# The first blocks of an encoder step: x and the modulation weights read by feature block, and three weight blocks begun on two of three token tiles

## The chip, the cores and the metric

The kernel runs on one core of a Trainium2 chip. Its engines work beside each other, each through an instruction queue of its own: TensorE (PE; its weight loads are listed as PEld), VectorE (DVE), ScalarE (ACT), GpSimd (POOL), and SyncE (SP), which issues most DMA transfers. They wait for one another by semaphores. What counts is the device time of one execution in microseconds. The time before is the median of three runs, 1598.21 us (1597.47 to 1599.44).

## The reference, cut to what matters

One inference step: one trunk layer on a prompt of 1024 tokens and on a sample of 32, with its own modulation row `c` for each of the two.

```python
mod = jax.nn.silu(c) @ w_ada + b_ada
sh1, sc1, gt1, sh2, sc2, gt2 = jnp.split(mod[:, None, :], 6, axis=-1)
h = rmsnorm(x, g_mix) * (1 + sc1) + sh1
u = h @ w_in
qa, ka, va, qm, km, vm, om, ip, fp, ga, gm = jnp.split(u, _split_points(), axis=-1)
...                    # band attention (qa, ka, va), mLSTM (qm .. fp), gates (ga, gm)
x = x + gt1 * (merged @ w_out)
...                    # rmsnorm, SwiGLU, residual, final rmsnorm
```

The change touches the part up to the first three column blocks of `u`: `rmsnorm` needs the mean square of each token over all 1024 features, and `sc1` and `sh1` need `silu(c) @ w_ada` over the first 2048 columns of `w_ada`.

## The kernel before, in words

Features lie on the 128 partitions, in eight blocks (`KD` = 8); tokens run along the free axis, 1024 of the prompt and then 32 of the sample, 1056 in all, in three tiles of 352 columns (`TILES`). A matrix product in f32 precision is made of three products of high and low parts (`PASSES`): weights and inputs are split into a high part (written by ACT) and the low remainder (by DVE or POOL). One weight block of 128 output columns on one tile therefore takes 8 x 3 products of 128x352. `unit()` (L436) makes these 24 for one tile and lets side work (attention, then the mLSTM) put its own instructions between them; `k` counts feature blocks.

**The front.** SP loads x by tokens: eight transfers of 128 tokens and one of the 32 sample tokens (L216 to L223). DVE sums the squares of each (L273), PE transposes x in 64 pieces of 128x128 (L281) and 8 of the sample, ACT copies the results into `xTs`. POOL takes the power -1/2 of the mean squares, and `bcast_cols` (L234) spreads the result over the partitions as `RB`. Then `load_ada` has eight transfers of 1 MB, rows of `w_ada` by input feature `k`. For each, PE adds the scale part into PSUM (L322, 128 columns wide, the two modulation rows side by side) and DVE accumulates the shift part in SBUF (L312, L314); at the end PE sums the shift over the partitions (`row_sums`, L348 and L352). Only with the eighth transfer is any scale known, for all feature blocks at once. `first_scale` and `first_shift` finish both; `scaled_x` (L375, DVE), `high_h` (L386, ACT) and `low_h` (L392 DVE for the prompt, L394 POOL for the sample's 32 columns) make the two parts of `h`. xT is also stored to DRAM (`xres`, L1508), and read back for the residual after attention.

**The first products.** `first_units` (L467) takes the first two weight blocks, K and V of head pair 0 (`KA`, `VA`), on all three tiles: 2 x 3 x 3 = 18 products for each `k`, 144 in all (L475), with one feature block at a time as `h` is made. The six sums fill six PSUM banks. Then Q of head pair 0 (`QA`) follows by `unit()`: 72 products (L443). After these come the blocks of head pair 1, with attention of pair 0 beside them as side work: scores (L725), bias added and maximum taken by DVE (L739), exponentials by ACT (L740) and scaled by POOL (L745), transposes (L752), products with V (L783).

**Orders and buffers.** The order on PE, ACT, DVE and POOL is that in which the code is written; the order of SP's transfers is chosen by a scheduler. Each weight block is loaded into one of three `wraw` buffers (512 KB; L419 via `weight`) and split into `wsp` or, where `home` is `slots`, elsewhere; early in the program the low part is POOL's (L410). A `wraw` buffer is free once its split is done, and a load that waits for one holds up what stands behind it in SP's queue. `W.loaded` and `W.split_n` count blocks loaded and split; `W.advance()` splits and loads as far as `W.ahead` and the buffers allow. The attention's bias tiles come from `rb_d` in DRAM (L691), and POOL clears two corners of each (L692, L693). DVE and ACT split the cached K and V of the sample (`cache_kv`: L684, L602, L603) as one of the jobs in `side.later`, which `unit()` takes one at a time.

Of the kernel before, what the change touches and what calls it, by code (L numbers as in the profile page):

```python
# [139 lines left out]
def hybrid_stream_step(  # L140
    ctx: ExitStack,
    tc: tile.TileContext,
    x_prompt, x_sample, cache_k, cache_v, state_conv, state_C, state_n, state_m,
# [9 lines left out]
    xp, xs_in = x_prompt[0], x_sample[0]  # L153
    w_in, w_ada, w_out, w_down = w_in[0], w_ada[0], w_out[0], w_down[0]
# [40 lines left out]
    def f(ap):  # L195
        return ap.bitcast(F32)
# [11 lines left out]
    ssq = cp.tile([P, NB], F32, name="ssq")  # L208
    pool.memset(ssq, 1.0)
# [4 lines left out]
    xtok = []  # L214

    for i in range(KD):  # L216
        if i % 2 == 0:
            xt = slot([P, 2, D])
            xtok += [xt[:, 0], xt[:, 1]]
        sp.dma_start(xtok[i], xp[i * P:(i + 1) * P])  # L220
    pool.dma_start(cols, params)
    xsm = tmpt((TS, D))
    sp.dma_start(xsm, xs_in)  # L223


# [23 lines left out]
    rstd = cp.tile([P, NB], F32, name="rstd")  # L249
    xres = dr.tile([KD, P, T], F32, name="xres")  # L250
    xTs, xTp, xns = [], [], []
    for j in range(KD):
        if j % 2 == 0:
            xT2 = slot([P, 2, T])
            xTp.append(xT2)
        xTs.append(xT2[:, j % 2])

    was = []
    first_ws, first_cols = [], (KA, VA)

    def load_ada(n):
        while len(was) < n:
            wa = slot([P, 2048])
            sp.dma_start(wa, w_ada[len(was) * P:(len(was) + 1) * P, 0:2048])
            was.append(wa)

    load_ada(KD)

    def square_sum(i):
        n = P if i < 8 else TS  # L270
        src = xtok[i] if i < 8 else xsm
        junk = tmpt((P, D), BF16)
        dve.tensor_tensor_reduce(junk[:n], src, src, 1.0, 0.0, ALU.mult, ALU.add, ssq[:n, i:i + 1])  # L273

    def x_transposes(g, j):

        pt = mmt()
        for n in range(2):
            for i in range(2):
                at = (2 * n + i) * P  # L280
                pe.transpose(pt[:, at:at + P], xtok[2 * g + i][:, (j + n) * P:(j + n + 1) * P], ident)  # L281
        act.activation(xTp[j // 2][:, :, g * 256:(g + 1) * 256], pt.rearrange("p (n t) -> p n t", n=2), AF.Copy)

    for g in range(4):
        for i in range(2):
            square_sum(2 * g + i)
        for j in range(0, KD, 2):
            x_transposes(g, j)
        if g == 2:
            param_cols()  # L290
    square_sum(8)
    for j0 in range(0, KD, 4):
        pt = mmt()
        for j in range(j0, j0 + 4):
            pe.transpose(pt[:, (j - j0) * TS:(j - j0 + 1) * TS], xsm[:, j * P:(j + 1) * P], ident[:TS, :TS])
        for j in range(j0, j0 + 4):
            act.activation(xTs[j][:, S:T], pt[:, (j - j0) * TS:(j - j0 + 1) * TS], AF.Copy)
    pool.tensor_scalar(ssq, ssq, 1.0 / D, EPS, op0=ALU.mult, op1=ALU.add)
    pool.tensor_tensor(rstd, ssq, mhalf[:, :NB], op=ALU.pow)
    RB = tmpt()  # L300

    psH, psA = ps_v(), ps_t()
    acv = [tmpt((P, D)) for _ in range(2)]
    sum_at = [psH, psA[:, 512:]]

    def shift_part(k, c, a, b):
        o, w, x = acv[c][:, a * P:b * P], was[k][:, a * P:b * P], csil[:, k, c:c + 1]  # L310
        if k == 0:
            dve.tensor_scalar(o, w, x, None, op0=ALU.mult)  # L312
        else:
            dve.scalar_tensor_tensor(o, w, x, o, op0=ALU.mult, op1=ALU.add)  # L314

    def first_ada():
        first_load()
        for k in range(KD):
            for b in range(KD):
                out = psA[:, b * P:(b + 1) * P]  # L320
                c = csil[:, k].unsqueeze(1).to_broadcast([P, DH, 2])
                pe.matmul(out.rearrange("p (r c) -> p r c", c=2), was[k][:, D + b * P:D + (b + 1) * P], c,  # L322
                          start=(k == 0 and b % 4 == 0), stop=(k == KD - 1), skip_group_check=True)
            if k < KD - 1:
                for c in range(2):
                    shift_part(k, c, 0, KD)
            else:
                shift_part(k, 0, 0, 2)
                shift_part(k, 1, 0, 2)
                shift_part(k, 0, 2, KD)  # L330
            if k == 0:
                bcast_cols(RB, rstd, [P] * 8 + [TS], 0)

    def first_load():

        for _ in range(2):
            first_ws.append(wraw.tile([P, KD, P], F32, tag="wraw", name=nm("wraw")))
        for half in range(2):
            for raw, c in zip(first_ws, first_cols):
                sp.dma_start(raw[:, 4 * half:4 * half + 4], w_in[512 * half:512 * half + 512, c:c + P].rearrange(  # L340
                    "(k p) c -> p k c", p=P))
        W.loaded = 2
        W.load(3)

    def row_sums(c, a, b):
        for b in range(a, b):
            at = (b % 4) * P + c * DH
            pe.matmul(sum_at[b // 4][:, at:at + DH], acv[c][:, b * P:(b + 1) * P],  # L348
                      ones[:, 0:1].to_broadcast([P, DH]), start=(c == 0 and b % 4 == 0), stop=True,
                      skip_group_check=True)  # L350
            if c == 1 and b >= 2:
                pe.matmul(sum_at[b // 4][:, at:at + DH], was[KD - 1][:, b * P:(b + 1) * P],  # L352
                          csil[:, KD - 1, 1:2].to_broadcast([P, DH]), start=False, stop=True, skip_group_check=True)
# [4 lines left out]
    def first_shift(a, b):
        p3 = sum_at[a // 4].rearrange("p (b c r) -> p c b r", c=2, r=DH)[:, :, a % 4:a % 4 + b - a, 0]
        dve.tensor_tensor(sh1[:, :, a:b], p3, cols[:, R_ADA + a:R_ADA + b].unsqueeze(1).to_broadcast([P, 2, b - a]),  # L360
                          op=ALU.add)
# [8 lines left out]
    def scaled_x(j, lo=0, hi=T):  # L370
        if j % 2 == 0 and lo == 0:
            xn2 = slot([P, 2, T])
            xns.extend([xn2[:, 0], xn2[:, 1]])
        for c, a, b in col_segments(lo, hi):
            dve.scalar_tensor_tensor(xns[j][:, a:b], xTs[j][:, a:b], s1[:, c, j:j + 1], RB[:, a:b], op0=ALU.mult,  # L375
                                     op1=ALU.mult)

    def high_h(j, lo=0, hi=T):

        if lo == 0:  # L380
            hs.append(slot([P, 2, T], F32R))
        for c, a, b in col_segments(lo, hi):
            x = xns[j][:, a:b]
            if c == 1:
                act.activation(x, x, AF.Identity, bias=sh1[:, c, j:j + 1])
            act.activation(hs[j][:, 0, a:b], x, AF.Identity, bias=sh1[:, c, j:j + 1] if c == 0 else 0.0)  # L386

    def low_h(j, lo=0, hi=T):
        for c, a, b in col_segments(lo, hi):
            x, o, h = xns[j][:, a:b], hs[j][:, 1, a:b], f(hs[j][:, 0, a:b])  # L390
            if c == 0:
                dve.scalar_tensor_tensor(o, x, sh1[:, c, j:j + 1], h, op0=ALU.add, op1=ALU.subtract)  # L392
            else:
                pool.tensor_tensor(o, x, h, op=ALU.subtract)  # L394
# [72 lines left out]
    def first_units(ws):  # L467

        S = ps_s()
        pts = [[mmt() for _ in TILES], [S[:, :512], S[:, 512:], psA[:, :512]]]  # L470
# [1795 lines left out]
```

## Time and profile before

| | us |
|---|---|
| median of three runs | 1598.21 |
| the profiled execution's own time | 1597.75 |
| its span in the trace | 1596.1 |
| x landed (end of the sample's transfer in the chain of waits) | 15.25 |
| w_ada landed (end of its piece of the chain) | 35.81 |

Read the profile as follows. All times count from the start of the span. A row of a group gives line, engine, operation, output and inputs by the program's names, shapes and count, then the busy time, the mean of one in ns, and the idle time before them with what ended it. A row of the timeline begins with start and duration; in brackets stands what the engine waited for. A piece of the chain of waits, which leads from the last instruction back to the first, gives start, duration and what ran. PE's matmuls are pipelined, so the last one of a burst shows a tail of some 0.3 us that the next work overlaps.

### The profile page before, as it was taken

Reading aid. Unit: us, or ns where it says so; the run is one execution under the profiler, and the core shown is the slowest. Engines: PE = TensorE matmul, PEld = TensorE weight load, DVE = VectorE, ACT = ScalarE, POOL = GpSimd, SP = SyncE. Lnnn points to the kernel's source line nnn. Section 1 sums busy time; section 2 is a strip of 40 time slices with the busy share of each in tenths; the row PEclk is TensorE's granted clock in tenths of the full one; section 3 lists DMA queues with packets and bytes.
Section 4 is the critical chain, followed back from the end, with each engine's and each line's share of the span. In section 5 each row is a group of like instructions: output and inputs, shape, how many; then the busy total and the mean of one; then the engine's idle time right before and its main releaser. Section 6 shows DMA issues by size and latency. Waiting matters only on the chain.

```text
span 1596.1 us, 27244 instructions
## 1 busy us (share of the span) xinstructions
PE 1566.1 (98%) x10167; PEld 1546.2 (97%) x10167; DVE 1126.4 (71%) x2291; ACT 790.5 (50%) x1735; POOL 420.0 (26%) x433
## 2 busy tenths in 40 slices
PE   7999999999999999999999999999999999999997
PEld 6989999999999999999999999999999999999997
DVE  7766555556776845546654699899888886799755
ACT  3665463544555545444433655544544444545443
POOL 0343242433222411000012100565565650000000
PEclk9999999999999999999999999999999999999999
DMA  9823323343132332675443311213222227427444
GB/s 364 265 83 94 98 82 109 86 135 110 43 94 67 88 86 75 133 257 176 133 145 112 106 54 54 95 57 103 81 80 94 68 78 252 143 80 249 130 136 155
DMA packets 209569, 193.48 MB, mean 121 GB/s; under 512 B 11530, under 2 KB 179118, under 8 KB 208414
## 3 DMA queue, kind: packets, MB, share of 16 engines
q1 hardware_dynamic: 206894, 189.92, 38.5%
q8 instruction: 80, 1.31, 0.4%
q10 hardware_dynamic: 2512, 1.77, 0.4%
q14 instruction: 51, 0.42, 0.1%
q0 software_dynamic: 32, 0.06, 0.0%
HBM read 153.24 MB, written 41.63 MB: 122 GB/s over the span
## 4 chain that ended last, share of the span: by engine, by line
PE 91%; DVE 3%; ACT 2%; DMA 2%; issue 1%; SPq 0%; POOL 0%; ACTq 0%; DVEq 0%; POOLq 0%
PE mm L443 41%; PE psb L1811 18%; PE mm L1811 11%; PE psb L2193 3%; PE mm L878 3%; PE mm L2193 2%; PE psV L783 2%; PE psb L2057 2%; PE psS L725 2%; PE psT L752 1%; DMA s<-in_w_ada_dram 1%; PE mm L2057 1%; DMA t<-in_x_sample_dram 1%; PE psV L1112 1%; PE mm L475 1%
## 5 line engine op out<-in xcount | busy, mean ns | idle before, releaser
L443 PE MATMUL mm<-s,wsp 128*128 128x352 f32 x4104 | 687.0, 324 | 0.0
L443 PEld LDWEIGHTS mm<-s,wsp 128*128 128x128 f32 x4104 | 657.3, 188 | 1.8 <-issue 0.4
L410 DVE TENSOR_TENSOR wsp<-wraw,wsp 128x512 fp32r<-128x512 f32 (+1 forms) x280 | 235.6, 858 | 114.1 <-ACT wsp L409 103.1
L1811 PE MATMUL psb<-s,wsp 128*128 128x352 f32 x1611 | 271.7, 322 | 1.6 <-DVE wsp L410 0.9
L409 ACT ACTIVATE wsp<-wraw 128x512 fp32r<-128x512 f32 x336 | 199.5, 617 | 142.4 <-PE psb L1811 44.5
L1811 PEld LDWEIGHTS psb<-s,wsp 128*128 128x128 f32 x1611 | 260.5, 188 | 2.1 <-DVE wsp L410 1.1
L1811 PE MATMUL mm<-s,wsp 128*128 128x352 f32 x933 | 159.3, 322 | 0.0
L1811 PEld LDWEIGHTS mm<-s,wsp 128*128 128x128 f32 x933 | 151.2, 188 | 0.5 <-DVE wsp L410 0.5
L745 POOL TENSOR_SCALAR st<-st,mx 128x640 f32<-128x640 f32 (+5 forms) x72 | 53.1, 738 | 186.2 <-DVE mx L744 171.2
L1207 DVE CUSTOM_DVE_ANT_0 junk<-wa,t 128x512 bf16<-128x512 f32 x128 | 94.7, 740 | 3.1 <-DMA wa<-in_w_mod_dram 2.1
L410 POOL TENSOR_TENSOR wsp<-wraw,wsp 128x512 fp32r<-128x512 f32 x56 | 74.9, 1357 | 57.1 <-ACT wsp L409 55.6
L739 DVE CUSTOM_DVE_ANT_0 st<-psS,bias 128x640 f32<-128x640 f32 (+5 forms) x72 | 44.5, 618 | 57.1 <-PE psS L725 41.9
L740 ACT ACTIVATE st<-st,mx 128x640 f32<-128x640 f32 (+5 forms) x72 | 47.9, 666 | 63.4 <-DVE mx L739 62.3
L1758 POOL TENSOR_TENSOR t<-t,sl 128x352 f32<-128x352 f32 x19 | 18.4, 969 | 212.8 <-ACT sl L1756 212.8
L759 ACT ACTIVATE pT<-psT 128x640 fp32r<-128x640 f32 (+3 forms) x80 | 38.7, 493 | 62.6 <-PE psT L752 47.6
L2166 POOL TENSOR_TENSOR fst<-fst,mhalf 128x6 f32<-128x6 f32 x1 | 2.3, 2312 | 221.1 <-DVE fst L2165 221.1
L764 DVE TENSOR_TENSOR pT<-psT,pT 128x640 fp32r<-128x640 f32 (+3 forms) x80 | 44.0, 558 | 22.2 <-ACT pT L759 22.2
L1420 POOL TENSOR_TENSOR wraw<-wraw,raw 128x512 f32<-128x512 f32 x33 | 55.8, 1705 | 0.9
L878 PE MATMUL mm<-s,s 128*128 128x264 f32 (+3 forms) x432 | 54.5, 283 | 0.0
L2193 PE MATMUL psb<-s,wsp 128*128 128x352 f32 x330 | 54.2, 324 | 0.0
L2193 PEld LDWEIGHTS psb<-s,wsp 128*128 128x128 f32 x330 | 53.1, 188 | 0.1
L878 PEld LDWEIGHTS mm<-s,s 128*128 128x128 f32 (+1 forms) x432 | 52.0, 179 | 0.5
(368 smaller groups left out, 2471.6 us busy)
## 6 DMA issues: line engine op xcount, KB each, us to landing
wraw<-in_w_in_dram SPq DMA_DIRECT2D x38, 512.0 KB, 4.0
wraw<-in_w_gate_up_dram SPq DMA_DIRECT2D x33, 512.0 KB, 3.9
wa<-in_w_mod_dram SPq DMA_DIRECT2D x64, 256.0 KB, 2.8
wraw<-in_w_down_dram SPq DMA_DIRECT2D x32, 512.0 KB, 4.3
a_d<-t SPq DMA_DIRECT2D x22, 528.0 KB, 2.7
g_d<-t SPq DMA_DIRECT2D x16, 528.0 KB, 3.2
x<-xres SPq DMA_DIRECT2D x16, 528.0 KB, 7.1
t<-g_d SPq DMA_DIRECT2D x16, 528.0 KB, 4.5
```

Of the source, the lines that this page charges most:

```text
L409: act.activation(dst[:, 0], src, AF.Copy)
L410: eng.tensor_tensor(dst[:, 1], src, f(dst[:, 0]), op=ALU.subtract)
L443: pe.matmul(pt[:, :hi - lo], wt[(w0 + k) // 4][:, a, (w0 + k) % 4], xt[k][:, b, lo:hi], start=(k == 0 and q == 0), stop=(k == n - 1 and q ...
L739: dve.tensor_tensor_reduce(so, sv, bi, -1.0, 3.0e38, ALU.add, ALU.min, mx[:n, 1:2])
L740: act.activation(st[:n, :w], st[:n, :w], AF.Exp, bias=mx[:n, 1:2], scale=-1.0, accum_out=mx[:n, 2:3])
L745: pool.tensor_scalar(st[:n, :w], st[:n, :w], mx[:n, 3:4], 1.0, op0=ALU.mult, op1=ALU.mult)
L878: pe.matmul(pt[:n, :wd], hs[k][:, a, i * P:i * P + n], whl[b][:, k, :wd], start=(k == 0 and q == 0), stop=(k == KD - 1 and q == 2))
L1207: dve.tensor_tensor_reduce(junk, wa, crow[:, c], 1.0, 0.0, ALU.mult, ALU.add, at)
L1420: self.eng.tensor_tensor(a(dst), a(x), a(y), op=op)
L1811: pe.matmul(acc, wt[:, a, k], x[k][:, b], start=(start and not onto and k == 0 and q == 0), stop=(stop and k == 3 and q == 2), skip_group_ ...
L2057: pe.matmul(acc, wt[k // 4][:, u, k % 4], piece_of[k, i][:, v], start=(k == 0 and q == 0), stop=(k == KP - 1 and q == 2))
L2193: pe.matmul(acc, wt[(k - k0) // 4][:, u, (k - k0) % 4], piece_of[k, 2][:, v], start=(k == 0 and q == 0), stop=(k == NF - 1 and q == 2))
```

## The change

The host hands over x already transposed, by feature block (`x`, [8, 128, 1056]), and `w_ada` by output feature block `j`, scale and shift apart (`[2, 8, 128, 1024]`; of the shift, blocks 0 to 2 are laid out as the scale is, blocks 3 to 7 with the output feature on the partition, so that a row can be summed along the free axis). So one block's scale and shift are known when that block's two transfers of 512 KB are in. The transposes of x and `xres`' stores are gone (x is read from the input at the end).

SP loads of each x block the first 704 tokens (`CUT`), then block 0 of `w_ada`, half of each of the first three weight blocks, blocks 1 and 2, the late 352 tokens, blocks 3 to 5, the other weight halves, blocks 6 and 7. Squares are ACT's, their addition DVE's, the sum over partitions PE's (`token_sums`). The scale sums of a block are 8 matmuls 128 columns wide (`scale_sums`); blocks 0 to 2 do the same for the shift, blocks 3 to 7 take two DVE reductions of 1024 (`shift_sums`). `first_units` makes K, V **and Q** on two tiles: again 3 x 2 x 3 = 18 products for each `k`, with the scale sums of block `k + 2` among them. The late tile of K and V (48 products) and of Q (24, by `unit()`) follow; `late_h` makes their `h` on the way, with the 32 sample columns by POOL in both steps.

```diff
-    for i in range(KD):
...
-        sp.dma_start(xtok[i], xp[i * P:(i + 1) * P])
+    CUT = TILES[2][0]
     for j in range(KD):
+        sp.dma_start(xTs[j][:, :CUT], x_t[j][:, :CUT])
...
+    def token_roots(t, n, at, r):
...
+        pool.tensor_tensor(x[:, 1], x[:, 0], mhalf[:, :3], op=ALU.pow)
+
+    def scale_sums(j, i=0):
+        at = P * (2 * i + j % 2)
+        for k in range(KD):
+            pe.matmul(psH[:, at:at + P].rearrange("p (r c) -> p r c", c=2), was[j][:, i, k * P:(k + 1) * P],
+                      csil[:, k].unsqueeze(1).to_broadcast([P, DH, 2]), start=(k == 0), stop=(k == KD - 1),
+                      skip_group_check=True)
+
+    def scale_done(j):
+        at = P * (j % 2)
+        act.activation(s1[:, :, j], psH[:, at:at + 2], AF.Identity, scale=gm1[:, j:j + 1], bias=gb1[:, j:j + 1])
+
+    def shift_sums(j, c):
+        dve.tensor_tensor_reduce(junk, was[j][:, 1], crow[:, c], 1.0, 0.0, ALU.mult, ALU.add, sha[:, c, j:j + 1])
+        act.activation(sh1[:, c, j:j + 1], sha[:, c, j:j + 1], AF.Identity, bias=cols[:, R_ADA + j:R_ADA + j + 1])
...
+    def first_units(put):
...
+        def late_h(k):
+            if 0 <= k < KD:
+                scaled_x(k, *late)
+            if 0 <= k - 1 < KD:
+                high_h(k - 1, *late)
+            if 0 <= k - 2 < KD:
+                low_h(k - 2, *late)
...
+        products(0, 2)
+        for j in range(KD):
+            square_sum(j, *late)
         for k in range(1, KD):
+            products(k, 0)
+            if k + 2 < KD:
+                scale_sums(k + 2)
+                scale_done(k + 2)
...
+            low_h(k, 0, CUT)
+            if k + 1 < KD:
+                scaled_x(k + 1, 0, CUT)
+                high_h(k + 1, 0, CUT)
...
+            if k + 2 < KD:
+                shift_sums(k + 2, 0)
+            products(k, 1)
...
+            if SHIFT_PE <= k + 1 < KD:
+                shift_sums(k + 1, 1)
+            if k >= 6:
+                late_h(k - 6)
+            products(k, 2)
+            if k == 5:
+                W.loaded = W.split_n = 3
+                W.load(6)
+        for k in range(2, KD + 2):
+            late_h(k)
             if k == 6:
-                W.advance()
+                put(*early[0], pts[0][0][:, :NT])
+        put(*early[1], pts[0][1][:, :NT])
+        for k in range(KD):
+            for q in range(3):
+                for i in range(2):
+                    product(k, i, q, 2)
...
     def units(w):
...
-            yield lo, hi, done[t] if done else unit(w, 0, hs, lo, hi)
+            if done is None or t in done:
+                yield lo, hi, done[t] if done else unit(w, 0, hs, lo, hi)
+            elif w is W.blocks[2]:
+                yield lo, hi, unit(w, 0, hs, lo, hi)
```

Three places show how instructions move. Below is PE at the front, before: a row of `psT<-csil` holds the scale sums for one input feature block, all eight output blocks; `psV<-ones` are the shift's row sums, `L475` the first products.

```order
L322 MATMUL psT_267<-csil,s_124 128x128 x8
L322 MATMUL psT_267<-csil,s_126 128x128 x8
L322 MATMUL psT_267<-csil,s_128 128x128 x8
L348 MATMUL psV_266<-ones,t_268 128x64 x2
L348 MATMUL psV_266<-ones,t_269 128x64 x2
...
L475 MATMUL mm_426<-s_432,wsp_398 128x352
L475 MATMUL psS_425<-s_432,wsp_400 128x352
L348 MATMUL psT_267<-ones,t_268 128x64
```

The same place after: `psV<-csil` are now the sums of one output block (s_112 block 0, s_118 block 1, s_121 block 2; x16 is scale and shift), and `L467` the products, of block 0 here.

```order
L325 MATMUL psV_153<-csil,s_112 128x128 x8
L467 MATMUL mm_263<-s_267,wsp_235 128x352
L467 MATMUL psS_154<-s_267,wsp_238 128x352
...
L325 MATMUL psV_153<-csil,s_118 128x128 x16
L467 MATMUL mm_263<-s_267,wsp_235 128x352
L467 MATMUL mm_264<-s_267,wsp_235 128x352
L467 MATMUL psS_154<-s_267,wsp_238 128x352 x2
...
L325 MATMUL psV_153<-csil,s_121 128x128 x16
```

The sums of block 0 stay ahead of the first product; those of blocks 1 to 7 have moved to between the products.

SP's queue at the start of attention, before: `bias` tiles, weight blocks (`wraw`), rows for later modulation (`wa`, `c_rows`) and small inputs.

```order
L419 DMA wraw_84_704<-in_w_in_dram 128x8x128
L561 DMA out_8_dram<-kf_81_683 128x32
...
L691 DMA bias_111_909<-rb_d_279 128x640
L1188 DMA wa_141_1084<-in_w_mod_dram 128x512
L691 DMA bias_178_1302<-rb_d_279 128x640
...
L419 DMA wraw_106_860<-in_w_in_dram 128x8x128
```

And after:

```order
L386 DMA wraw_50_706<-in_w_in_dram 128x8x128
L602 DMA out_2_dram<-kf_47_628 128x512
...
L386 DMA wraw_60_782<-in_w_in_dram 128x8x128
L733 DMA bias_71_851<-rb_d_163 128x640
L1230 DMA wa_105_1041<-in_w_mod_dram 128x512
L733 DMA bias_142_1259<-rb_d_163 128x640
```

The first row of each is the load of the seventh weight block, `wraw_106_860` and `wraw_60_782` that of the eighth: both bias tiles stood ahead of the eighth, and now stand behind it.

DVE at the first two score steps, before: `L684`, `L602` and `L603` with `s_835` split the cached K and V, `L739` with `st` adds the bias to a score and takes its maximum.

```order
L684 TENSOR_TENSOR s_835<-t_709,s_835 64x512 x2
L602 CAST s_835<-t_709 128x8x64
L603 TENSOR_TENSOR s_835<-t_709,s_835 128x8x64
L624 TENSOR_TENSOR s_720<-t_717,s_716 64x352 x2
L558 TENSOR_TENSOR s_852<-mm_862,s_852 64x352 x2
L739 ISA st_914,mx_915<-psS_913,bias_909 128x128
...
L739 ISA st_935,mx_936<-psS_934,bias_909 128x256
```

And after (`L780` is what L739 was, `L726`, `L645`, `L646` what the three splits were):

```order
L646 TENSOR_TENSOR s_794<-mm_814,s_794 128x8x64
L595 TENSOR_TENSOR s_831<-mm_784,s_831 64x352 x2
L780 ISA st_856,mx_857<-psS_855,bias_851 128x128
...
L726 TENSOR_TENSOR s_881<-t_716,s_881 64x512 x2
L645 CAST s_881<-t_716 128x8x64
L646 TENSOR_TENSOR s_881<-t_716,s_881 128x8x64
L780 ISA st_892,mx_893<-psS_891,bias_851 128x256
```

The cache's splits stood ahead of the first score's reduction, and now stand between the first and the second.

More of the change, by code (lines that the diff above doesn't have):

```diff
@@ L258, in hybrid_stream_step @@
+    first_ws = [wraw.tile([P, KD, P], F32, tag="wraw", name=nm("wraw")) for _ in first_cols]
     was = []
[L259 to L273, printed above, removed]
@@ L291, in hybrid_stream_step @@
[L291 to L299, printed above, removed]
-    RB = tmpt()
@@ L305, in hybrid_stream_step @@
[L305 to L353, printed above, removed]
+    def load_ada():
+        j = len(was)
+        wa = slot([P, 2, D])
+        for i in range(2):
+            sp.dma_start(wa[:, i], w_ada[i, j])
+        was.append(wa)
@@ new lines, in load_first @@
+    def load_first(half):
+        for raw, c in zip(first_ws, first_cols):
+            sp.dma_start(raw[:, 4 * half:4 * half + 4], w_in[512 * half:512 * half + 512, c:c + P].rearrange(
+                "(k p) c -> p k c", p=P))
+    crow = slot([P, 2, D])
+    sq2 = slot([P, 2, T])
+    load_ada()
+    load_first(0)
+    load_ada()
+    load_ada()
+    for i, xp in enumerate(xTp):
+        sp.dma_start(xp[:, :, CUT:], x_t[2 * i:2 * i + 2].rearrange("n p t -> p n t")[:, :, CUT:])
+    for _ in range(3, 6):
+        load_ada()
@@ L355, in hybrid_stream_step @@
+    load_first(1)
+    for _ in range(6, KD):
+        load_ada()
+    SHIFT_PE = 3
+    RB = tmpt()
+    junk = tmpt((P, D), BF16)
+    gb1 = cp.tile([P, KD], F32, name="gb1")
+    sha = cp.tile([P, 2, KD], F32, name="sha")
     sh1 = cp.tile([P, 2, KD], F32, name="sh1")
     s1 = cp.tile([P, 2, KD], F32, name="s1")
[L358 to L361, printed above, removed]
@@ new lines, in silu_cols, with square_sum, token_sums @@
+    def silu_cols():
+        act.activation(csil, cols[:, R_C:R_C + 16].rearrange("p (c k) -> p k c", c=2), AF.Silu)
+        dve.scalar_tensor_tensor(gb1, cols[:, R_ADA + 8:R_ADA + 16], 1.0, gm1, op0=ALU.add, op1=ALU.mult)
+    def square_sum(j, lo, hi):
+        n = hi - lo
+        o = sq2[:, j % 2, :n] if j else acc[:, :n]
+        act.activation(o, xTs[j][:, lo:hi], AF.Square)
+        if j:
+            dve.tensor_tensor(acc[:, :n], acc[:, :n], o, op=ALU.add)
+    def token_sums(a0, n, at, r):
+        for i, a in enumerate(range(0, n, P)):
+            b = min(a + P, n)
+            pe.matmul(tok[:b - a, at + r * i:at + r * (i + 1)], acc[:, a:b], ones[:, 0:1].to_broadcast([P, r]),
+                      start=(i == 0), stop=True, skip_group_check=True)
@@ L465, in first_low @@
         dve.tensor_tensor(lo, first_ws[i][:, 4 * half:4 * half + 4], f(hi), op=ALU.subtract)
-    def first_units(ws):
-        S = ps_s()
-        pts = [[mmt() for _ in TILES], [S[:, :512], S[:, 512:], psA[:, :512]]]
-        wts = [w[3] for w in ws]
+    def first_units(put):
+        early, late = TILES[:2], TILES[2]
+        for j in range(2):
+            square_sum(j, 0, CUT)
+        silu_cols()
+        rows = silu_rows()
+        for j in range(2, KD):
+            square_sum(j, 0, CUT)
+        token_sums(0, CUT, 0, DH)
+        for i, p in enumerate(rows):
+            act.activation(crow[:, i // 2, (i % 2) * 512:(i % 2 + 1) * 512], p, AF.Silu)
+        scale_sums(0)
+        groups = [(0, 3 * P), (3 * P, CUT)]
+        for i, (lo, hi) in enumerate(groups):
+            token_roots(i, hi - lo, 3 * DH * i, DH)
+        for i in range(2):
+            first_high(i, 0)
+        scale_done(0)
+        for i, (lo, hi) in enumerate(groups):
+            bcast_cols(RB, roots[:, 1, 3 * i:3 * i + 3], [min(P, hi - a) for a in range(lo, hi, P)], lo)
+        scale_sums(0, 1)
+        shift_done(0)
+        first_high(2, 0)
+        pts = [[mmt(), mmt()], [psS[:, :512], psS[:, 512:]], [psA[:, :512], mmt()]]
+        last = [tok, psH]
@@ L473, in product, with products @@
         def product(k, i, q, t):
             (a, b), (lo, hi) = PASSES[q], TILES[t]
-            pe.matmul(pts[i][t][:, :hi - lo], wts[i][k // 4][:, a, k % 4], hs[k][:, b, lo:hi],
+            out = last[i] if t == 2 else pts[i][t]
+            pe.matmul(out[:, :hi - lo], W.blocks[i][3][k // 4][:, a, k % 4], hs[k][:, b, lo:hi],
                       start=(k == 0 and q == 0), stop=(k == KD - 1 and q == 2))
-        for t, (lo, hi) in enumerate(TILES):
+        def products(k, q):
+            for i in range(3):
+                for t in range(2):
+                    product(k, i, q, t)
@@ L506, in first_units @@
[L506 to L520 removed]
+                token_sums(late[0], NT, NT, 32)
@@ L521, in first_units @@
+        for k in range(KD):
+            for q in range(3):
+                for i in range(2):
+                    product(k, i, q, 2)
+        first[id(W.blocks[0])] = {2: last[0][:, :NT]}
+        first[id(W.blocks[1])] = {0: pts[1][0][:, :NT], 1: pts[1][1][:, :NT], 2: last[1][:, :NT]}
+        first[id(W.blocks[2])] = {0: pts[2][0][:, :NT], 1: pts[2][1][:, :NT]}
+        for w, n in zip(W.blocks, (3, 3, 2)):
+            for _ in range(n):
                 W.used(w)
+        W.advance()
     def units(w):
@@ L1496, in hybrid_stream_step @@
         W.add(w)
[L1499 to L1509 removed]
+    first_units(segs[0][1][0].put)
     W.ahead = 2
```

232 lines of the change are left out of this document (111 added, 121 removed).

## The prediction

> **What bounds the kernel now.** I read the head of the page, then the chain of work that ended last, then the busy times in stretches of the first 130 us.
>
> ```profile
> span 1596.1 us, 27244 instructions
> PE 1566.1 (98%) x10167; PEld 1546.2 (97%) x10167; DVE 1126.4 (71%) x2291; ACT 790.5 (50%) x1735; POOL 420.0 (26%) x433
> PE 91%; DVE 3%; ACT 2%; DMA 2%; issue 1%; SPq 0%; POOL 0%; ACTq 0%; DVEq 0%; POOLq 0%
> ```
>
> PE is busy for 98% of the span and 91% of the chain that sets the end. A change helps only where PE waits, or does work that isn't a product. The chain shows where that is, and the stretches (PE, weight load, DVE, ACT and POOL busy; clock; DMA share; GB/s) show how much:
>
> ```profile
> 4.70 10.55 DMA t<-in_x_sample_dram
> 15.26 20.55 DMA s<-in_w_ada_dram
> 35.86 2.05 PE psT L322 x16
> ...
> 912.41 52.19 PE mm L443 x324
> ```
>
> ```profile
> 40.90:68.50 27.60, 26.85 (x166) 25.57 (x167) 25.84 (x36) 17.07 (x38) 8.18 (x10) 1.00 0.82 281
> 68.50:86.90 18.40, 18.40 (x117) 18.08 (x117) 10.61 (x18) 12.85 (x28) 10.23 (x12) 1.00 0.77 234
> 86.90:110.00 23.10, 20.22 (x131) 19.27 (x130) 12.66 (x34) 15.11 (x31) 7.51 (x11) 1.00 0.21 58
> 5.00:15.00 10.00, 7.90 (x52) 7.18 (x52) 8.45 (x15) 7.13 (x13) 0.00 (x0) 1.00 1.03 388
> 40.97 0.43 PE L475 MATMUL mm<-s,wsp 128*128 128x352 f32 x1 [0.66 <-ACT s L386]
> ```
>
> Loading sets the start: x until 15.26, w_ada until 35.81, the first product at 40.97. Until then PE has only transposes and scale sums, in the shadow of the loads. From 40.9 on PE hardly waits. So the early start is the prize, and what PE does between 41 and 87 is the price. One product costs 52.19/324 = 0.161 us.
>
> **Term 1, the first product.** Eight early parts of x, 128x704 in f32, are 2.88 MB. All of x, 4.33 MB, took until 15.26; at 388 GB/s that is 11.2 us, so transfers ran from 4.1. At that rate the early x is in at 11.5. The two loads of w_ada's block 0 (1.05 MB) and three half weight blocks (0.79 MB) follow until 16.2. What then stands in line:
>
> ```profile
> L2152 ACT ACTIVATE t<-x 128x704 f32<-128x704 f32 x7 | 5.5, 781 | 5.8 <-DVE x L2146 5.8
> L2154 DVE TENSOR_TENSOR t<-t,t 128x704 f32<-128x704 f32 x7 | 6.2, 886 | 0.3 <-ACT t L2152 0.3
> L2173 DVE SCALAR_TENSOR_TENSOR x<-x,gcols,t 128x704 f32<-128x704 f32 x8 | 7.4, 946 | 0.0
> L348 PE MATMUL psT<-ones,t 128*128 128x64 f32 x16 | 2.9, 260 | 0.0
> L1138 POOL TENSOR_TENSOR dn<-dn,mhalf 128x2 f32<-128x2 f32 x16 | 12.1, 759 | 1.3
> L322 PE MATMUL psT<-csil,s 128*128 128x128 f32 x128 | 16.2, 279 | 3.1 <-DMA s<-in_w_ada_dram 3.1
> ```
>
> The last square 0.8 and its addition 0.9; six two-pass token sums 1.5 (L348's eight pairs: 2.9, their tail included); POOL's two powers of three columns, 0.9 each (L1138's two columns took 0.76), and 0.2 ahead of them on DVE; block 0's shift sums 1.8 (L322's sixteen took 2.05 with a last one's 0.28 as tail, so 0.11 an instruction), and ahead of them six transposes 0.6. Then the same tail as before, from the last sums through scale, first tile and its high part: 40.97 - 35.86 - 2.05 = 3.1. In all 11.5 + 10.7 = 22.2: **-18.8**. It can be 20.5 if sums and powers overlap, 25 if x comes at the later stretch's 281 GB/s (2.9 more).
>
> **Term 2, from the first product to the end of the first 144.** Before, 27.6 us for 144 products (23.2), some row sums and short waits (4.4 together). After, the same 144 products stand in three blocks of two tiles, but the sums of w_ada go along between them: 2 groups for each of blocks 1 and 2, one for each of 3 to 7, nine in all at 1.8 = 16.2, and late token sums and transposes 1.0. Before, these sums cost nothing, since PE waited for w_ada anyway (L322: "3.1 <-DMA"). That cover is gone: **PE pays 16.2 of the 18.8 back here**. Waits come on top. DVE's sum in this stage is about 34:
>
> ```profile
> L273 DVE CUSTOM_DVE_ANT_0 t<-s 128x1024 bf16<-128x1024 f32 x8 | 9.7, 1225 | 6.2 <-DMA s<-in_x_prompt_dram 6.0
> L410 DVE TENSOR_TENSOR wsp<-t,wsp 128x512 fp32r<-128x512 f32 x32 | 22.0, 686 | 2.4 <-ACT wsp L409 2.3
> L410 DVE TENSOR_TENSOR s<-x,s 128x352 fp32r<-128x352 f32 x68 | 33.4, 535 | 2.4 <-ACT s L409 2.4
> ```
>
> That is 15 passes over 704 columns (0.95) 14.2, ten shift sums over 1024 12.3, six weight parts 4.1, seven late additions 3.7. PE's 40.4 is longer, yet each block goes DVE, ACT, DVE, PE in turn. I take 1.8 where seven late additions stand in DVE's queue between block 0 and block 1; 0.55 twice where one PSUM bank is read by ACT while PE has the next sums for it; and 0.45 for each of six blocks: 5.6. No row shows these waits; their bounds are 1.9 (what the 4.4 holds now beside eleven row-sum pairs at 0.22) and 9. So 46.0 - 27.6 = **+18.4**, and the 144 end at 68.2, where they end now.
>
> **Term 3, the next 72 products.** Before, 72 of block QA, without a wait (18.40 of 18.40). After, 48 for the late tile and 24 of QA. DVE's late parts take 0.93 for one k, POOL's two sample parts 2 x 0.59 = 1.18, PE's six products 0.97:
>
> ```profile
> L394 POOL TENSOR_TENSOR s<-s,s 128x32 fp32r<-128x32 f32 x8 | 4.7, 592 | 38.2 <-ACT s L386 36.6 <-DMA xres<-s 1.7
> ```
>
> POOL is the slower by 0.2 for each of eight: **+1.5**, between 0.5 (started two early) and 3.
>
> **Term 4, the first steps of attention.** The three blocks now end together, and 48 products fewer stand between Q's late output and the first scores. Three things come due there. First, the bias tile. SP's queue now has it behind the load of the eighth weight block, which needs the buffer that POOL frees with the fifth block's split:
>
> ```profile
> 71.72 2.55 POOL L410 TENSOR_TENSOR wsp<-wraw,wsp 128x512 fp32r<-128x512 f32 x2 [5.91 <-ACT wsp L409]
> 74.33 1.99 POOL L636 MEMSET s<- 64x1056 f32 x2
> 77.24 0.47 SPq L691 DMA_DIRECT2D bias<-rb_d  x1
> 87.95 0.39 SPq L419 DMA_DIRECT2D wraw<-in_w_in_dram  x1
> L645 POOL TENSOR_SCALAR s<-s 64x352 fp32r<-64x352 f32 x24 | 14.4, 602 | 10.8 <-ACT s L643 9.6
> wraw<-in_w_in_dram SPq DMA_DIRECT2D x38, 512.0 KB, 4.0
> bias<-rb_d SPq DMA_DIRECT2D x2, 320.0 KB, 7.0
> ```
>
> Before, the bias was asked for at 77.24, ten us ahead of that load. After, POOL has a split 2.55, clears 1.99, six query parts 3.6 and a split 2.55 to do from about 77 on (68.2, 48 products, 1.5), so 88 to 89 with a wait for ACT between; the bias lands 4.0 to 7.0 later, at 92 to 96, and POOL then clears two corners (0.3). I take 94. PE's second scores stand at
>
> ```profile
> 87.14 0.34 PE L725 MATMUL psS<-s,s 128*128 128x128 f32 x2
> 90.30 0.50 PE L725 MATMUL psS<-s,s 128*128 128x256 f32 x2 [0.86 <-DVE mx L739]
> 84.49 0.60 DVE L602 CAST s<-t 128x512 fp32r<-128x512 f32 x1
> 85.12 1.66 DVE L603 TENSOR_TENSOR s<-t,s 128x512 fp32r<-128x512 f32 x1
> 92.23 0.48 POOL L745 TENSOR_SCALAR st<-st,mx 128x256 f32<-128x256 f32 x1 [0.71 <-DVE mx L744]
> PE psV L783 <- ACT pT L759: 1.7, 1, 1.7
> PE psS L725 <- DVE mx L739: 0.9, 1, 0.9
> PE psT L752 <- DVE pT L764: 0.3, 1, 0.3
> ```
>
> and the same 114 products (72, then 42) precede them, so 91: a wait of 3.2. Second, K's low part and the first scores: 0.8. Third, DVE now splits the caches (L602 and L603 alone 2.3) between the first reduction and the second: what the bias doesn't hide, 1.2. The two steps that follow then each show their chain from score to weighted row (90.30 to 92.71 here, 2.3), 4.6, since PE's products that covered it have been issued. 9.8, less the 2.9 in the three waits above: **+6.9**. Bounds 0 (bias in time, cover as before) and 11.
>
> **Edits that I cost at nothing.** The x transposes (L281), x's store and its reading back lay under loads; the read now comes from the input, as many bytes. The host's new layout isn't timed.
>
> **Sum.** -18.8 + 18.4 + 1.5 + 6.9 = +8.0, on the profiled execution's own 1597.75 (span 1596.1 and 1.65 around it; 0.03% under the median of the runs): **1605.7 us**.
>
> [...] L394's 128x32 subtraction took 0.26 us with DVE idle and 0.88 beside its long operations:
>
> ```profile
> 50.05 0.26 POOL L394 TENSOR_TENSOR s<-s,s 128x32 fp32r<-128x32 f32 x1 [3.06 <-ACT s L386]
> 60.25 0.88 POOL L394 TENSOR_TENSOR s<-s,s 128x32 fp32r<-128x32 f32 x1 [1.67 <-DMA xres<-s]
> ```
>
> [...]
>
> **Rivals.**
> - *The early start is kept* (other side: faster). Term 2's waits are only 1.9, DVE hands over in time, the late tile runs at PE's pace, and the bias lands before 91. Then -18.8 + 14.7 + 0 + 0 = -4.1: 1593.7. For it: PE is the longer sum in term 2 by 6. Against: DVE's queue has shift sums and late additions ahead of what PE needs. It decides at POOL's split of the fifth block ending before 84, seven us ahead of the second scores.
> - *No change*: the bias arrives in time, terms 1 to 3 as forecast, term 4 only +1: +2.1, 1599.9.
> - *POOL is held up by DVE*: sixteen late sample parts at 0.88 instead of 0.59 (4.6 on POOL), less what the bias wait hides: some 5 more than forecast, 1611.
> - *It doesn't do what it says*: loads of 128x704 and 512-byte rows come at 281 GB/s or less, the first product is at 25, and the rest holds: 1608.5.
>
> **How the numbers follow.** Forecast 0.60 (1601 to 1610, by half of each bound), early start kept 0.15, no change 0.13, POOL held up 0.08, slow loads 0.04. The range 1597 to 1611.5 leaves out the faster case and the tail of POOL's, 0.2. A measurement can tell about 0.2%, 3.2 us, from no change: below 1595 is the faster case alone, 0.15; 1595 to 1601.4 no change and the low edge of the forecast, 0.15; the rest, 0.70, is slower.
>
> **What would show it.** First product at 20.5 to 25; end of the first 144 products between 64 and 71, with waits for ACT and DVE there; the last late-tile product and the 24 of QA without a wait above 0.5; the bias landing at 92 to 96, and PE waiting behind it for the first reduction. I am wrong if PE reaches 68 with over 144 products done, or if the window from 86.9 to 110 keeps its 20 us of busy PE.

## The result and the profile after

The changed kernel takes 1607.46 us (median of six, 1607.17 to 1608.65), the kernel before 1598.62 us in the same runs (1597.47 to 1599.48): a ratio of 1.0057, interval 1.0044 to 1.0070, 8.8 us slower. The forecast was 1605.7.

The head of the page after, with the shares of the chain of waits by engine:

```profile
span 1605.4 us, 27215 instructions
PE 1566.3 (98%) x10133; PEld 1546.2 (96%) x10133; DVE 1113.5 (69%) x2296; ACT 800.6 (50%) x1757; POOL 416.6 (26%) x439
PE 88%; DVE 4%; ACT 3%; DMA 3%; issue 1%; POOL 0%; SPq 0%; ACTq 0%; DVEq 0%; POOLq 0%
```

PE is busy for the same 1566 us and the span is 9.3 longer, so all of it is PE waiting or having nothing to do (its work changed too: fewer instructions, and some of them slower). PE's share of the chain falls from 91% to 88%; DVE, ACT and transfers take what it loses. The two stages that the change rewrote, as stretches (columns as in the prediction):

```profile
24.36:70.72 46.36, 42.55 (x297) 40.33 (x298) 32.90 (x53) 19.91 (x46) 3.15 (x6) 1.00 0.69 241
70.72:84.13 13.41, 11.78 (x75) 11.52 (x73) 8.72 (x19) 12.49 (x35) 7.91 (x15) 1.00 0.00 1
```

The first is from the first product to the end of the 144, the second the 72 that follow. PE's timeline at the seams, each row with its wait in brackets:

```profile
14.00 2.77 PE L307 MATMUL psT<-ones,t 128*128 128x64 f32 x12 [6.04 <-DVE t L302]
16.70 3.59 PE L325 MATMUL psV<-csil,s 128*128 128x128 f32 x16
20.13 0.91 PE L227 MATMUL mm<-ident,roots 128*128 128x128 f32 x6
20.97 2.05 PE L325 MATMUL psV<-csil,s 128*128 128x128 f32 x16
24.36 0.43 PE L467 MATMUL mm<-s,wsp 128*128 128x352 f32 x1 [1.35 <-ACT s L357]
...
40.59 0.80 PE L307 MATMUL psT<-ones,t 128*128 128x32 f32 x6 [1.76 <-DVE t L302]
...
77.96 0.40 PE L467 MATMUL psT<-s,wsp 128*128 128x352 f32 x1 [1.63 <-DVE s L366]
...
91.86 0.33 PE L766 MATMUL psS<-s,s 128*128 128x128 f32 x2
...
97.28 0.50 PE L766 MATMUL psS<-s,s 128*128 128x256 f32 x2 [2.97 <-DVE mx L780]
97.62 4.60 PE L410 MATMUL mm<-s,wsp 128*128 128x352 f32 x18
```

Two things stand out. The first sixteen scale-sum instructions (L325) take 3.59 us, the next sixteen of the same kind 2.05: PE ran at little more than half its pace. And 18 products right behind the 2.97 wait take 4.60, where 18 take 3.05 nine us later: two thirds of the pace.

Three rows more, the first two of PE before (the end of its 144 products and the sixth score), the third the sixth score after:

```profile
68.52 5.55 PE L443 MATMUL mm<-s,s 128*128 128x352 f32 x33
103.52 0.83 PE L725 MATMUL psS<-s,s 128*128 128x320 f32 x4
...
113.88 0.83 PE L766 MATMUL psS<-s,s 128*128 128x320 f32 x4
```

Against before, stage by stage: the first product comes 16.6 earlier (24.36 for 40.97); the 144 products take 46.4 for 27.55 (40.97 to 68.52), +18.8; the next 72 take 13.4, where 72 at 0.161 are 11.6 (the transposes that stood among them before come later now), +1.8. That makes +4.0 when 216 products are done. At the sixth score, with the same work done, it is +10.4, so the first steps of attention cost 6.4. PE's last instruction is 10.1 later; the span is only 9.3 longer, since it ends 8.7 behind that instruction for 9.5 before.

### The profile page after: what moved, and what is told of

Its sections match the earlier page's. It is cut to its first block, busy times and chain, and to the rows that moved or that the text cites. A ratio compares the mean times of both kernels' runs of the same rounds, so it can differ in the third digit from the quotient of the medians.

```text
span 1605.4 us, 27215 instructions
## 1 busy us (share of the span) xinstructions
PE 1566.3 (98%) x10133; PEld 1546.2 (96%) x10133; DVE 1113.5 (69%) x2296; ACT 800.6 (50%) x1757; POOL 416.6 (26%) x439
## 4 chain that ended last, share of the span: by engine, by line
PE 88%; DVE 4%; ACT 3%; DMA 3%; issue 1%; POOL 0%; SPq 0%; ACTq 0%; DVEq 0%; POOLq 0%
PE mm L410 40%; PE psb L1843 18%; PE mm L1843 10%; PE psb L2225 3%; PE mm L920 3%; PE mm L2225 2%; PE psV L825 2%; PE psb L2089 2%; DMA s<-in_w_ada_dram 2%; PE psS L766 1%; PE psT L793 1%; PE mm L2089 1%; DMA s<-in_x_dram 1%; PE psV L1154 1%; PE psT L1156 1%
## 5 line engine op out<-in xcount | busy, mean ns | idle before, releaser
L780 DVE CUSTOM_DVE_ANT_0 st<-psS,bias 128x640 f32<-128x640 f32 (+5 forms) x72 | 44.5, 618 | 60.8 <-PE psS L766 43.6
L1790 POOL TENSOR_TENSOR t<-t,sl 128x352 f32<-128x352 f32 x19 | 18.4, 966 | 212.8 <-ACT sl L1788 212.8
```

The costliest lines, as they stand in the source:

```text
L780: dve.tensor_tensor_reduce(so, sv, bi, -1.0, 3.0e38, ALU.add, ALU.min, mx[:n, 1:2])
```

## Experiments

All compare with the kernel before on the same chip; what an edit did inside is read from its trace, by four marks on PE: the first product, the end of the 144, the first product of QA's late tile, and the sixth score.

| kernel | first | end of 144 | QA late | sixth score | time |
|---|---|---|---|---|---|
| before | 40.97 | 68.52 | - | 103.52 | 1598.62 (6) |
| changed | 24.36 | 70.72 | 80.28 | 113.88 | 1607.46 (6 runs) |
| e1_warm | 23.18 | 69.55 | 79.11 | 112.95 | 1607.82 (4) |
| e10_warm52 | 22.61 | 68.97 | 78.53 | 112.46 | 1605.70 (1) |
| e3_late | 26.26 | 76.58 | 86.14 | 120.26 | 1613.10 (4) |
| e8_late2 | 25.21 | 69.01 | 78.58 | 112.88 | 1607.56 (1) |
| e4_sums | 25.14 | 64.07 | 73.64 | 108.06 | 1601.48 (1) |
| e2_bias | 25.42 | 72.83 | 82.39 | 112.66 | 1607.35 (4) |
| e5_bias_put | 24.60 | 70.93 | 79.21 | 110.00 | 1607.20 (1) |
| e6_bias_cache | 24.89 | 71.26 | 80.82 | 108.47 | 1603.62 (1) |
| e9_all | 22.72 | 66.47 | 74.75 | 102.91 | 1599.41 (11) |
| e11_best | 21.94 | 64.23 | 72.47 | 100.63 | 1596.05 (11) |

The first product alone moves by 1.9 us between kernels that are the same up to there (24.36 to 26.26 without the extra transposes; in e3_late ACT waited 1.3 for the second part of x), so differences between marks tell more than the marks, and one run's time tells little under 2 us. Nor does a mark come through whole: e9_all's sixth score is 11.0 earlier than the changed kernel's, its profiled execution 7.0 shorter.

### PE's pace before the first product

```diff
+        for i in range(36):       # e10_warm52: 52
+            pe.transpose(psH[:, (i % 4) * P:(i % 4 + 1) * P], cols[:, R_C:R_C + 1].to_broadcast([P, P]), ident)
         token_sums(0, CUT, 0, DH)
```

> The changed kernel with 36 extra transposes on PE between the transposes of the silu rows and the token sums, into a bank that the first scale sums overwrite. In the changed kernel the twelve token-sum instructions took 2.77 us (0.23 each) and block 0's sixteen scale-sum instructions 3.59 (0.22 each), where the same sixteen take 2.05 a little later. Theory (PE was idle for 6 us before them and runs at half its pace until it has worked for some us): token sums about 1.5, scale sums about 2.0, the first product 2 to 3 us earlier than 24.36, the whole 2 to 3 us shorter than the changed kernel. Rival (transfers that land in those microseconds slow PE's reads): the durations stay at 2.8 and 3.6, first product and time unchanged or later.

> The changed kernel with 52 extra transposes ahead of the token sums instead of the 36 of e1_warm, so that no gap stays before them; nothing else. Theory (PE falls back to half its pace in the 1.8 us gap that e1_warm left): token sums 1.4 to 1.6 and block 0's first scale sums 2.0 to 2.1, the first product 1.5 to 2.5 earlier than the changed kernel counted from the last addition of squares, all of it in the time. Rival (it was the other changes of e9_all that brought this): scale sums 3.4 or more.

With 36, PE's extra work ended 1.84 us ahead of the token sums, which took 1.71; but the scale sums behind them took 3.45. The first product was 1.2 earlier, and the median of four runs, 1607.82, shows nothing of it. With 52 only 0.59 us were left open. PE's timeline of e10_warm52:

```profile
14.36 1.56 PE L307 MATMUL psT<-ones,t 128*128 128x64 f32 x12 [0.59 <-DVE t L302]
15.84 2.05 PE L325 MATMUL psV<-csil,s 128*128 128x128 f32 x16
...
22.61 0.43 PE L469 MATMUL mm<-s,wsp 128*128 128x352 f32 x1 [1.35 <-ACT s L357]
```

Token sums 1.56 for 2.77, scale sums 2.05 for 3.59, and the first product 8.25 us behind the start of the token sums for 10.36: 2.1 us. The only thing changed is that PE had work before, so its idling set the pace. The same sixteen scale sums took 3.59 us with 6.04 us of idling ahead of the token sums (the changed kernel), 3.45 with 1.84 (e1_warm, at a granted clock of 0.56 between 15.7 and 19.0) and 2.05 with 0.59.

### The late tile's squares

In the changed kernel, DVE's additions of the late squares stand between block 0 and block 1. DVE's timeline:

```profile
36.23 4.30 DVE L302 TENSOR_TENSOR t<-t,s 128x352 f32<-128x352 f32 x7 [7.48 <-ACT s L300]
```

DVE had waited 7.5 us for ACT, and then PE waited for DVE. First I put the squares off, behind block 2's scaling, with the late sums and roots one block later (e3_late):

> The changed kernel with the squares and additions of the late tile moved behind the low part of block 1 and the scaling of block 2, and the late token sums and roots one block later. Theory (seven additions stand in DVE's queue between block 0 and block 1 and cost PE the 1.76 us that it waits at 38.8): that wait goes, the first 144 products end 1.5 to 2 us earlier, the time is as much shorter than the changed kernel. Rival (DVE's 34 us of work are what paces this stage): the wait comes back at blocks 2 and 3, and the time is unchanged.

It cost 4 us in this stage (50.3 for 46.4). PE's waits in e3_late (line, what it waited for, us in total, times, longest):

```profile
PE psT L307 <- DVE t L302: 8.8, 2, 7.2
PE psT L467 <- DVE roots L318: 3.0, 1, 3.0
```

The wait came back one block later (1.65 of the first row), and a second one with it: token sums and a product of QA share one PSUM tile, so the product waited until DVE, behind other work, had read the sums. The theory's cure was wrong, not its place. Then I brought the squares forward, into the time in which ACT and DVE were idle:

```diff
         high_h(1, 0, CUT)
+        for j in range(4):
+            square_sum(j, *late)
         products(0, 1)
         scale_sums(2)
         scale_done(2)
+        for j in range(4, 7):
+            square_sum(j, *late)
         scale_sums(2, 1)
         shift_done(2)
+        square_sum(7, *late)
         products(0, 2)
-        for j in range(KD):
-            square_sum(j, *late)
```

> The changed kernel with the squares of the late tile brought forward instead of put off: four behind block 1's high part, where ACT and DVE are idle (DVE waits 7.5 us there), the others around the sums of block 2. Theory: the 1.76 us wait ahead of the late token sums goes, and no other comes; the stage from the first product to the end of the 144 takes 44.3 to 45 instead of 46.4. Rival (ACT is held up with block 2's scale and shift, and PE's next sums wait for their PSUM bank): the stage stays above 46.

The stage took 43.8 for 46.4, and the waits for the late additions and their roots (1.76 and 0.34 in the changed kernel) were gone. The time didn't follow: the first product came 0.85 later in that run, and 0.7 went into a longer wait for the bias (3.69 for 2.97).

### The sums among the products

This kernel leaves out PE's sums for blocks 1 to 7; all blocks take block 0's scale, and blocks 1 and 2 its shift.

```diff
     def scale_sums(j, i=0):
+        if j:
+            return
```

> The changed kernel without PE's sums for blocks 1 to 7 (seven groups for the scale, two for the shift): every block uses block 0's scale, and blocks 1 and 2 its shift. Theory (these nine groups are the price on PE that the stage pays, 16.2 us, and DVE's 34 us are the next bound): the stage from the first product to the end of the 144, 46.4 us in the changed kernel, comes to 35 to 38, so 8 to 11 shorter; about as much in the whole time. Rival (the groups only fill waits for h): the stage stays above 43.

The stage, as a stretch of e4_sums:

```profile
25.14:64.07 38.93, 29.03 (x153) 25.48 (x154) 32.81 (x53) 19.23 (x46) 3.15 (x6) 0.96 0.79 279
```

38.9, just above what I expected: 7.4 less for 16.2 of sums. DVE's timelines show which groups counted, two rows of the changed kernel and then three of e4_sums (one line lower in its source):

```profile
40.45 0.94 DVE L366 SCALAR_TENSOR_TENSOR s<-s,sh,s 128x704 fp32r<-128x704 f32 x1
66.61 1.22 DVE L334 CUSTOM_DVE_ANT_0 t<-s,s 128x1024 bf16<-128x1024 f32 x1
...
29.59 4.30 DVE L302 TENSOR_TENSOR t<-t,s 128x352 f32<-128x352 f32 x7 [2.17 <-ACT s L300]
33.80 0.95 DVE L367 SCALAR_TENSOR_TENSOR s<-s,sh,s 128x704 fp32r<-128x704 f32 x1
59.95 1.22 DVE L335 CUSTOM_DVE_ANT_0 t<-s,s 128x1024 bf16<-128x1024 f32 x1
```

DVE's additions of the late squares begin 11.9 us behind the first product in the changed kernel (at 36.23) and 4.4 in e4_sums. The four groups of blocks 1 and 2 stand ahead of them; they are the 7.4. From block 1's low part (L366) to the stage's last shift sum (L334), DVE takes 26.16 us with the other five groups on PE and 26.15 without, and the stage ends 4.1 behind that in both. So the five groups of blocks 3 to 7, 9 us of PE's work, cost nothing: DVE, which waits for ACT's weight parts on the way, takes as long. Theory and rival are each right for a part: four groups are paid for, five fill time in which PE would wait.

### Bias, caches and K's first tile

```diff
         sp.dma_start(rb_d, bass.AP(...))
+        for h in range(2):
+            early_bias[h] = bias_load(h)
         return ckv
```

> The changed kernel with the first two bias tiles asked for as soon as their source is written, so that they stand in SP's queue ahead of the eighth weight block's load. Theory (the bias tile's late landing at 96.7 holds up the first score's reduction, and PE's 18 products after that wait run at a slower pace, 4.60 us instead of 2.90): the wait of 2.97 at the second scores goes, the slow products with it, and the time is 3 to 5 us shorter than the changed kernel. Rival (the scores wait for DVE, which splits the caches there, and for the queries' low parts): another wait of 2 to 3 us stands at the same place, and the time is within 1 us of the changed kernel.

From QA's late tile to the sixth score it takes 30.3 for 33.6, so 3.3 less, as the theory had it. The time hardly shows it, 1607.35: e2_bias' first product was 1.1 late in the profiled execution, and its 144 products took another 1.05 longer, at a granted clock of 0.84 behind the same 1.75 us wait that cost the changed kernel nothing more. PE's waits of 0.85 and 1.38 at the third scores and second transposes stayed. Next I put the caches' splits off as well (e6_bias_cache), or K's first tile (e5_bias_put):

```diff
-                side.later.append(lambda: cache_kv(ckv))
+                side.later += [lambda: None] * 8 + [lambda: cache_kv(ckv)]
```

> The early bias tiles of e2_bias, and the splits of the cached K and V put off by some steps, behind the fifth score's reduction. Theory (with the bias in time, the second score's reduction waits for DVE, which splits the caches from 97.5 to 100.0 there): PE's waits of 0.85 and 1.38 at the third scores and the second transposes go, 2 us less than e2_bias counted from the first product. Rival (each step's own chain, from score to weighted row, has lost its cover): waits of together 2 us stay at these places.

PE's timeline of e6_bias_cache shows both steps without a wait, and 18 products in 3.05:

```profile
94.68 0.40 PE L773 MATMUL psS<-s,s 128*128 128x256 f32 x2
94.92 3.05 PE L410 MATMUL mm<-s,wsp 128*128 128x352 f32 x18
97.80 0.27 PE L800 MATMUL psT<-ident,st 128*128 128x128 f32 x1
97.83 0.59 PE L773 MATMUL psS<-s,s 128*128 128x384 f32 x2
98.26 2.09 PE L410 MATMUL mm<-s,wsp 128*128 128x352 f32 x12
100.24 0.41 PE L800 MATMUL psT<-ident,st 128*128 128x128 f32 x2
```

From QA's late tile to the sixth score it is 27.65 now, 5.95 less than in the changed kernel. That is nearly all of the 6.4 that this part had cost.

```diff
-            if k == 6:
-                put(*early[0], pts[0][0][:, :NT])
+        put(*early[0], pts[0][0][:, :NT])
         put(*early[1], pts[0][1][:, :NT])
```

> The early bias tiles of e2_bias, and K's first tile written out after the late tile's h is made instead of in the middle of it. Theory (the 1.63 us that PE waits in the late tile's products comes from K's subtraction standing in DVE's queue, where it waits for ACT, and not from POOL's sample parts): that wait goes, and 1.5 us of it stay in the time against e2_bias. Rival (POOL's sample parts set the pace): the wait stays, 1 us or more.

The late tile's 48 products take 8.28 for 9.56, and the 1.63 is gone; the next part gives back 0.5 (30.8 for e2_bias' 30.3). The time, of one run, shows nothing of it, 1607.20, although the sixth score is 3.9 earlier than in the changed kernel. Some of it was lost to PE's pace behind that mark: 18 products behind the next wait of 1.74 took 4.26, for 3.04 behind 1.73 in the changed kernel. DVE's timeline in the changed kernel shows whose wait it was:

```profile
75.72 1.06 DVE L595 TENSOR_TENSOR s<-mm,s 64x352 fp32r<-64x352 f32 x2 [1.39 <-ACT s L590]
76.80 0.55 DVE L347 SCALAR_TENSOR_TENSOR s<-s,s,t 128x320 f32<-128x320 f32 x1
77.27 1.47 DVE L366 SCALAR_TENSOR_TENSOR s<-s,sh,s 128x320 fp32r<-128x320 f32 x3
```

K's subtraction waits for ACT's copy, and the parts that PE needs stand behind it.

### All of it, and three edits more

> All of these on the changed kernel: 52 extra transposes ahead of the token sums (so many that PE isn't idle until x is in), the late squares brought forward, K's first tile written out later, the bias tiles asked for early, the caches' splits put off. Theory: first product at 21.5 to 22.5 (2 to 3 less than 24.4), 1.5 from the late squares, 1.5 from K, 3 to 5 from bias and caches: 8 to 11 less than the changed kernel's 1607.5, so 1596.5 to 1599.5, level with before or up to 2 us under it. Rival (what one wait gives up another takes): 1601 or more.

1599.41 over 11 runs, ratio 1.0005 (0.9996 to 1.0014): level with before, where the changed kernel was 0.57% above. What stays in its stage of 144 products (43.75) is DVE waiting for weight parts behind shift sums, and PE's shift sums of block 2. e11_best adds:

```diff
-    SHIFT_PE = 3
+    SHIFT_PE = 2                      # and the host's layout: range(3) -> range(2)
...
+        shift_sums(2, 0)
         for j in range(4):
...
-        scale_sums(2, 1)
-        shift_done(2)
...
+            if 1 <= k <= 3:
+                first_high(k - 1, 1)
             if k + 2 < KD:
                 shift_sums(k + 2, 0)
```

and QA's `first_high(2, 0)` behind block 0's first tile.

> e9_all with three more edits in the stage of the first 144 products: block 2's shift by two DVE reductions instead of 16 PE instructions, the high parts of the second weight halves ahead of the shift sums on ACT (DVE waits 0.9 us for each there), and QA's first high part behind block 0's first tile. Theory: PE gives up 1.8 us of sums and 0.6 of waits for the bank, DVE 0.9 for each of three blocks, so the stage takes 41 to 42.5 instead of 43.75, and the time is 1.5 to 3 less than e9_all: 1596.5 to 1598, at or below before. Rival (DVE, with 2.5 us more to do, now paces the stage): the stage stays above 43, the time at 1599 or more.

1596.05 (1594.84 to 1597.04, 11 runs) for 1597.96, ratio 0.9987 (0.9978 to 0.9996): 1.9 us faster than before. The stage, as a stretch of e11_best:

```profile
21.94:64.23 42.29, 40.27 (x281) 38.53 (x282) 35.62 (x57) 20.20 (x48) 4.79 (x6) 1.00 0.80 281
```

PE is busy for 40.3 of 42.3. DVE took on 2.7 us more; for that it comes to block 3's first shift sum 1.0 earlier than in e9_all, counted from the first product, and waits 1.4 for weight parts instead of 3.0. It still sets the end, as in the changed kernel. This is its last shift sum of the stage, and the stage ends 4.1 behind it, as it did there:

```profile
60.11 1.22 DVE L334 CUSTOM_DVE_ANT_0 t<-s,s 128x1024 bf16<-128x1024 f32 x1
```

## Why the prediction was right

**Term 1, -18.8 forecast, -16.6 measured: mis-sized.** The 2.2 are lost in two places. The token sums start at 14.0 and not at 13.2 (11.5 and 1.7): DVE's additions, seven at almost 1 us each, set the pace there, and ACT waited 0.2 for DVE before each of the last four squares, not for x.

```profile
7.98 5.87 DVE L302 TENSOR_TENSOR t<-t,s 128x704 f32<-128x704 f32 x6 [1.24 <-ACT s L300]
```

From there to the first product it takes 10.4 for the forecast's 9.0. Two pieces were slow, as PE had been idle for 6 us: the token sums, 2.77 for 1.5, and block 0's scale sums, for which the forecast has no term, 3.59 for the 2.05 of a full pace. e10_warm52 shows that the two cost 2.1. A third piece was priced too high, from the last sums to the first product, 1.35 for 3.1; without that the term would be further off. The rows that I took prices from stood where PE had hardly been idle, L322's behind x's transposes, work that this change removes, and L348's behind L322's.

**Term 2, +18.4 forecast, +18.8 measured: right in size, its largest part only half right in cause.** The wait of 1.8 for the late additions was 1.76 (e8_late2 removes it), the two for a PSUM bank 0.45 each; of the 2.7 for handing over six blocks, PE shows 0.7. But the 16.2 are not all PE's price, as the prediction had it. e4_sums shows that the four groups of blocks 1 and 2 are, 7.4 us; while PE does the other five, DVE takes 26.2 us with them or without. The prediction put DVE's 34 aside because PE's 40.4 was the longer sum. From block 1 on the two are almost equally long (in e2_bias, where PE was slower, DVE's stretch grew to 27.2), and that PE's sum alone gave the measured end is partly luck.

**Term 3, +1.5 forecast, +1.8 measured: right in size, wrong in cause.** POOL's sample parts take 0.37 and 0.45 us in that stage, not 0.59 each, so POOL needs 0.82 for one k where PE needs 0.97. The wait was DVE's, 1.63 us behind K's output (e5_bias_put), and with it the prediction's sign of no wait above 0.5 failed. The groups of POOL between 66 and 82 us, in the trace after:

```profile
L368 POOL TENSOR_TENSOR s<-s,s 128x32 fp32r<-128x32 f32 x8 | 3.0, 372 | 24.4 <-ACT s L360 24.4
L349 POOL TENSOR_TENSOR s<-s,t 128x32 f32<-128x32 f32 x5 | 2.2, 449 | 0.0
```

With it falls the rival of POOL being held up by DVE; how a longer POOL operation would fare there wasn't tried. The prediction's row for POOL beside an idle DVE was misread, too: at 50.05, where L394 took 0.26, DVE was at work (DVE's timeline before).

```profile
48.91 1.45 DVE L375 SCALAR_TENSOR_TENSOR s<-s,s,t 128x1024 f32<-128x1024 f32 x2
50.27 1.27 DVE L392 SCALAR_TENSOR_TENSOR s<-s,sh,s 128x1024 fp32r<-128x1024 f32 x1
```

So 0.26 and 0.88 both stand beside DVE, and what makes the two differ is not shown.

**Term 4, +6.9 forecast, +6.4 measured: the mechanism right, one part wrong.** The trace after shows SP's load behind POOL's split, and the bias behind it (SP's queue, POOL's and DVE's timelines):

```profile
89.09 2.52 POOL L377 TENSOR_TENSOR wsp<-wraw,wsp 128x512 fp32r<-128x512 f32 x2
91.64 0.38 SPq L386 DMA_DIRECT2D wraw<-in_w_in_dram  x1
92.07 0.66 SPq L733 DMA_DIRECT2D bias<-rb_d  x1
96.75 0.14 POOL L734 MEMSET bias<- 64x64 f32 x1 [5.13 <-DMA bias<-rb_d]
96.93 0.29 DVE L780 CUSTOM_DVE_ANT_0 st<-psS,bias 128x128 f32<-128x128 f32 x1 [3.36 <-POOL bias L734]
```

The bias landed at 96.7, just behind the forecast's 92 to 96, and PE's wait was 2.97 for 3.2. The 4.6 for two steps without cover did not come: with bias and caches in time (e6_bias_cache) PE waits for neither step. In its place stood what I hadn't priced, 18 products at two thirds of the pace, 4.60 for 3.05, and of the 2.9 that the forecast took off, the wait of 1.7 for ACT is still there, behind the sixth score as before. That the term came so near is partly luck. The cover of 48 products was no loss by itself; the transfers and DVE work that had fitted under it were.

The rivals: the early start was not kept, but e11_best shows that some of it can be, 1.9 us where the rival had 4.1. The bias' place, on which it was to decide, is worth 3.3 (e2_bias), with the caches 5.95. No change would have needed the bias in time. The loads came at 369 GB/s between 4 and 14 us, near the 388 taken and not at 281; that the first product is near the slow loads' 25 has the reasons given for term 1.

## What to carry to other kernels

Work on the critical engine that looks free under a transfer has a price once the transfer no longer covers it, but only where no other engine takes as long (four groups of sums cost 7.4 us here, five nothing): add up both before moving the start, stretch by stretch, and leave work out of one to see which of them sets the end. When a block of work is brought forward, look at what used to land under it: here a small transfer behind a buffer's release in a queue whose order nobody wrote. And take an operation's price from a row where the engine has been as busy as it will be: sixteen scale sums took 3.59 us behind 6 us of idling and 2.05 a little later.

## What the runs showed of the hardware that I had not expected

PE lost its pace after some short waits in these runs and kept it after others. A wait of 1.76 us was followed by a granted clock of 1.00 between 36 and 47 us in the changed kernel, and one of 1.75 in front of the same work by 0.84 between 37 and 48 us in e2_bias; behind a wait of 1.73 us, 18 products took 3.04 in the changed kernel, and behind one of 1.74 they took 4.24 in e9_all. At the start of the changed kernel the profile's granted clock reads 1.00 for a stretch in which sixteen scale sums take 3.59 us for 2.05 (in e1_warm it reads 0.56 where they take 3.45); behind the wait for the bias it reads 0.65, where 18 products take 4.60 for 3.05. Two stretches of the changed kernel, 16.7 to 20.1 and 97.3 to 102.2:

```profile
16.70:20.10 3.40, 3.40 (x17) 3.40 (x17) 0.28 (x3) 2.12 (x4) 1.69 (x2) 1.00 1.03 411
97.30:102.20 4.90, 4.90 (x22) 4.88 (x23) 3.67 (x10) 2.11 (x6) 0.41 (x1) 0.65 0.08 18
```
